# First norm of a streaming encoder step: sums of squares on another engine, smaller token tiles, loads in another order, sums in other PSUM banks

## The chip, the cores and the metric

One Trainium2 chip, one core. The metric is the device time of one execution, in microseconds (us); the program is one launch. The engines are TensorE (PE; its weight loads are PEld), VectorE (DVE), ScalarE (ACT), GpSimd (POOL) and SyncE (SP), which here only issues transfers (DMAs). Each engine works through its own queue in order.

## The reference

One layer of a streaming encoder, for 2048 prompt tokens and 32 sample tokens of width 1024:

```python
shift_m, scale_m, gate_m, shift_f, scale_f, gate_f = adaln_modulation(c, w_ada, b_ada)   # silu(c) @ w_ada + b_ada
h = rmsnorm(x, g_pre_mix) * (1.0 + scale_m) + shift_m                                     # the first norm
z = h @ w_in                        # one projection for both mixers and their gates
...                                 # chunk-band attention, gated linear attention, merge, w_out
x = x + gate_m * rmsnorm(merged @ w_out, g_post_mix)
...                                 # second norm, MLP with a causal convolution
```

All is float32. Only the first norm and the modulation that it needs (`shift_m`, `scale_m`) are touched here; the rest of the layer follows it and is about 95% of the time.

## The kernel before, in words

Everything is held transposed: 1024 channels are 8 chunks (`k`, `KD = 8`) of 128 partitions, tokens lie along the free dimension. The 2080 tokens are 5 blocks of 416 (`NB`), each of two halves of 208 (`NH`), so there are ten halves, `hb` 0 to 9. A product in float32 is made of three matmuls (`mm3`, lines 78 to 80): each operand is split into a high part (ACT) and a low part (DVE).

The first stage does these things at once:

- `ada_load(j, v)` and `ada(j, v)`: the modulation. Four pairs of loads of `w_ada` (1 MB each, tile `wa`, six buffers) give scale (`v = 1`) and shift (`v = 0`) for chunks `2j` and `2j + 1`. TensorE multiplies (L315), DVE copies the result to `mr` (L318), TensorE sums it (L322), DVE adds bias and gain (`mod_finish`, L134 and L138).
- `prep_load(hb)`: loads a half's 8 chunks as two tiles `xk` of 4 chunks (L262), six buffers.
- `prep_stats(hb, add)`: ACT squares two chunks at a time into `sq` or `sq2` (L271, L274; one buffer of `sq2`), and the engine `add` sums them (L275, L276): VectorE for halves 0 and 1, GpSimd for 2 to 9. Then `rstd_bcast` splits the sum (`sh` on ACT, `sl` on DVE, L69 and L72); its second part, `finish`, sums over partitions with two matmuls by ones (L148, L149) into a PSUM tile `pst`, and makes `rstd` (ACT L154, L155; DVE L156 to L158).
- `prep_apply(hb, r, ks)`: for each chunk, multiplies by scale and `rstd` (DVE, L294), adds the shift and rounds to the high part `hi` (ACT, L295), and makes the low part `lo` (DVE, L296), into `hA` or, past column 1664, `hB`. In half 2 the odd chunks go another way: GpSimd multiplies by the scale (`prep_scale`, L283) and by `rstd` (L292).
- `w_pieces`: two weight matrices of 256 columns, each in four pieces of two chunks (tile `wr`, two buffers, L185); ACT makes `wh` (L186), DVE `wl` (L187).
- `wave(b, ks, ps)`: the projection of block `b` by these weights, 4 outputs, chunk by chunk: 12 matmuls a chunk into four PSUM tiles `px`. `wave_evac` copies them out (`tx`, L225 on ACT, L228 on DVE) and stores them.

PSUM has two pools: `psm` with two banks, used by the stages after this one, and `psx` with six, whose tag `px` is shared here by the waves, `ada` and `pst`.

Only TensorE is in the order in which the code is written (`manual_schedule`). For the other engines and the DMA queues the framework's planner chooses the order at compile time, by readiness with its own costs, among what the buffers allow. TensorE's order for block 0 is: sums of halves 0 and 1 and the first four `ada`, then wave steps 0 to 7 with an `ada` before each of steps 1 to 4, the sum of half 2 ahead of step 4 and that of half 3 ahead of step 7. For the blocks after it there is a loop over `s_` from 2 to 9: four wave steps each, and after the first of them the sum of half `s_ + 2`, whose `prep_apply` follows; `prep_load(s_ + 4)` and `prep_stats(s_ + 3)` stand at the head.

After it, `n_tile` (L517) makes projections with tokens as rows; in its loop a side stream makes bias tables and the other modulation values.

Of the kernel before, what the change touches and what calls it, by code (L numbers as in the profile page):

```python
# [10 lines left out]
F32 = mybir.dt.float32  # L11
# [3 lines left out]
OP = mybir.AluOpType  # L15
# [5 lines left out]
KD = 8  # L21
TP, TS = 2048, 32
T = TP + TS
# [16 lines left out]
def dap(ap, offset, dims):  # L40
    return bass.AP(tensor=ap.tensor, offset=ap.offset + offset, ap=dims)


def f32(ap):
    return ap.bitcast(F32)


def parts(c0, n):

    out = []  # L50
    if c0 < TP:
        out.append((0, min(n, TP - c0), 0))
    if c0 + n > TP:
        out.append((max(0, TP - c0), n, 1))
    return out
# [3 lines left out]
def encoder_step(ctx: ExitStack, tc: tile.TileContext, I, O):  # L59
    nc = tc.nc  # L60

    def pool(st, name, bufs=1, **kw):
        return st.enter_context(tc.tile_pool(name=name, bufs=bufs, reuse_waits="tile", **kw))
# [3 lines left out]
    def split(hi, lo, src, keep=False):  # L67

        i = nc.scalar.activation(hi, src, AF.Copy)  # L69
        if keep and not in_order[0]:  # L70
            tc.keep_in_program_order(i)
        nc.vector.tensor_sub(lo, src, f32(hi))  # L72
# [22 lines left out]
    mod = consts.tile([128, 6, KD, 2], F32, name="mod")  # L95
# [44 lines left out]
    def rstd_bcast(pl, pps, tag, s, n, w, bufs=1):  # L140

        sh = pl.tile([128, w], F32R, name="sh", tag="sh")
        sl = pl.tile([128, w], F32R, name="sl", tag="sl")
        split(sh[:, :n], sl[:, :n], s)

        def finish():
            p = pps.tile([128, 512], F32, name="pst", tag=tag)
            nc.tensor.matmul(p[:, :n], ones, sh[:, :n], start=True, stop=False)  # L148
            nc.tensor.matmul(p[:, :n], ones, sl[:, :n], start=False, stop=True)  # L149

            r0 = pl.tile([128, w], F32, name="rst0", tag="sh")
            t = pl.tile([128, w], F32, name="rstt", tag="sl")
            r = pl.tile([128, w], F32, name="rstd", tag="rstd", bufs=bufs)
            nc.scalar.activation(r0[:, :n], p[:, :n], AF.Ln, bias=eps, scale=1.0 / D)  # L154
            nc.scalar.activation(r0[:, :n], r0[:, :n], AF.Exp, scale=-0.5)  # L155
            nc.vector.scalar_tensor_tensor(t[:, :n], p[:, :n], D * EPS, r0[:, :n], op0=OP.add, op1=OP.mult)  # L156
            nc.vector.scalar_tensor_tensor(t[:, :n], t[:, :n], -0.5 / D, r0[:, :n], op0=OP.mult, op1=OP.mult)
            nc.vector.scalar_tensor_tensor(r[:, :n], t[:, :n], 1.5, r0[:, :n], op0=OP.add, op1=OP.mult)  # L158
            return r[:, :n]

        return finish
# [9 lines left out]
    def h_at(x, k, c0, n):  # L171
        return hA[x][:, k, c0:c0 + n] if c0 < TA else hB[x][:, k, c0 - TA:c0 - TA + n]
# [3 lines left out]
    psm = pool(mix, "psm", bufs=2, space=PSUM)  # L176
# [14 lines left out]
    def load_w(wp, c0, n, w, kp, wr=2):  # L191
        hl_, steps = w_pieces(wp, c0, n, w, kp, wr)
        for f in steps:
            f()
        return hl_
# [40 lines left out]
    NH = 208  # L236
    late_w = {}
    with ExitStack() as st:
        stg = pool(st, "stgA", bufs=2, side="right")
        wp = pool(st, "wN", bufs=2, side="right")  # L240
        psx = pool(st, "psx", bufs=6, space=PSUM)
        prep = st.enter_context(ExitStack())
        pp = pool(prep, "prep", side="right")
# [9 lines left out]
            nc.vector.tensor_add(sel, sel, ident[:, 32 * j:32 * j + 2])  # L253

        XK = {}
        POOL = {2: (1, 3, 5, 7)}

        def prep_load(hb, q_=nc.sync):
            XK[hb] = []
            for k in range(0, KD, 4):  # L260
                x = pp.tile([128, 4, NH], F32, name="xk", tag="xk", bufs=6)
                q_.dma_start(x, dap(I["xT"], k * 128 * T + NH * hb, [[T, 128], [128 * T, 4], [1, NH]]))  # L262
                XK[hb].append(x)

        def prep_stats(hb, add):

            sq = pp.tile([128, 2, NH], F32, name="sq", tag="sq", bufs=2)
            for k in range(0, KD, 2):
                x = XK[hb][k // 4][:, k % 4:k % 4 + 2]
                if k == 0:  # L270
                    nc.scalar.activation(sq, x, AF.Square)  # L271
                    continue
                s2 = pp.tile([128, 2, NH], F32, name="sq2", tag="sq2")
                nc.scalar.activation(s2, x, AF.Square)  # L274
                add.tensor_add(sq, sq, s2)  # L275
            add.tensor_add(sq[:, 0], sq[:, 0], sq[:, 1])  # L276
            return lambda: rstd_bcast(pp, psx, "px", sq[:, 0], NH, NH, 2)

        def prep_scale(hb):
            for k in POOL.get(hb, ()):  # L280
                for a, e, s in parts(NH * hb, NH):
                    xs = XK[hb][k // 4][:, k % 4, a:e]
                    nc.gpsimd.tensor_scalar(xs, xs, mod[:, 1, k, s:s + 1], 1.0, op0=OP.mult, op1=OP.mult)  # L283

        def prep_apply(hb, r, ks_=range(KD)):
            for k in ks_:
                for a, e, s in parts(NH * hb, NH):
                    hi, lo = [h_at(x, k, NH * hb + a, e - a) for x in range(2)]
                    xs = XK[hb][k // 4][:, k % 4, a:e]
                    s1, s2 = mod[:, 1, k, s:s + 1], mod[:, 0, k, s:s + 1]  # L290
                    if k in POOL.get(hb, ()):
                        nc.gpsimd.tensor_mul(xs, xs, r[:, a:e])  # L292
                    else:
                        nc.vector.scalar_tensor_tensor(xs, xs, s1, r[:, a:e], op0=OP.mult, op1=OP.mult)  # L294
                    nc.scalar.activation(hi, xs, AF.Identity, bias=s2)  # L295
                    nc.vector.scalar_tensor_tensor(lo, xs, s2, f32(hi), op0=OP.add, op1=OP.subtract)  # L296

# [2 lines left out]
        def ada_load(j, v):  # L300

            PIECE[j, v] = []
            for half in range(2):
                w = pa.tile([128, 4, 256], F32, name="wa", tag="wa", bufs=6)
                nc.sync.dma_start(w, dap(I["w_ada"], half * 512 * 6 * D + v * D + 256 * j,
                                         [[6 * D, 128], [128 * 6 * D, 4], [1, 256]]))
                PIECE[j, v].append(w)
# [28 lines left out]
        def wave(b, ks_, ps, chunks=range(4)):  # L336
            for k in ks_:
                for i in chunks:
                    mm3(ps[i][:, :NB], [t_terms(w0[i // 2], 128 * (i % 2), b, k)], first=k == 0, last=k == KD - 1)

        def wave_tiles():
            return [psx.tile([128, 512], F32, name="px", tag="px") for _ in range(4)]

        def wave_evac(b, ps):
            for i in range(4):
                t_evac(stg, first[i // 2][0], i % 2, b, ps[i][:, :NB])

        fin0 = prep_stats(0, nc.vector)()
        ada_load(1, 1)
        for s_ in steps:  # L350
            s_[0]()
        ada_load(1, 0)
        m0 = ada(0, 1)
        r0 = fin0()
        fin1 = prep_stats(1, nc.vector)()
        m1 = ada(0, 0)
        m0()
        r1 = fin1()
# [1 line left out]
        fins = {}  # L360
        for s_ in steps:
            s_[1]()
        ada_load(2, 1)
        prep_load(2)
        m0 = ada(1, 1)
        m1()
        m1 = ada(1, 0)
        m0()
        ada_load(2, 0)
        ada_load(3, 1)  # L370
        prep_load(3)
        prep_apply(0, r0, [0, 1])
        prep_apply(1, r1, [0, 1])
        for s_ in steps:
            s_[2]()
        ada_load(3, 0)
        fins[2] = prep_stats(2, nc.gpsimd)
        wave(0, (0, ), ps)
        m1()
        m0 = ada(2, 1)  # L380
# [5 lines left out]
        wave(0, (1, ), ps)  # L386
        m0()
        m1 = ada(2, 0)
        fins[3] = prep_stats(3, nc.gpsimd)
        wave(0, (2, ), ps)  # L390
        m1()
        m0 = ada(3, 1)
# [1 line left out]
        prep_apply(1, r1, [4, 5])  # L394
        wave(0, (3, ), ps)
        m0()
        prep_scale(2)
        m1 = ada(3, 0)
        r2 = fins.pop(2)()()
        wave(0, (4, ), ps)  # L400
# [8 lines left out]
        r3 = f3()  # L409
        wave(0, (7, ), ps)  # L410
        prep_apply(3, r3)
        fins[4] = prep_stats(4, nc.gpsimd)
        wave_evac(0, ps)
        ada_st.close()
        arena2 = pool(ar2, "arena2")
# [1 line left out]
        for s_ in range(2, 10):  # L417
            b = s_ // 2
            if s_ + 4 < 10:
                prep_load(s_ + 4)  # L420
            if s_ + 3 < 10:
                fins[s_ + 3] = prep_stats(s_ + 3, nc.gpsimd)
            k0 = 4 * (s_ % 2)
            if s_ + 2 < 10:
                fin = fins.pop(s_ + 2)()
            if s_ % 2 == 0:
                ps = wave_tiles()
            if b < 4:
                wave(b, range(k0, k0 + 1), ps)
                prep_apply(s_ + 2, fin())  # L430
                wave(b, range(k0 + 1, k0 + 4), ps)
            elif s_ % 2 == 0:

                wave(b, range(KD), ps, (0, 1))
                wn = load_w(wp, 2048, 256, 272, 2, 2)
            else:
                wave(b, range(KD), ps, (2, 3))
            if s_ % 2:
                wave_evac(b, ps)
# [160 lines left out]
    with ExitStack() as st:  # L600
# [20 lines left out]
        for p in range(2):  # L621
            for x, sb in (("P", SBP), ("S", SBS)):
                s_ = gp.tile([128, 2, 128], F32, name=f"SB{x}{p}")
# [209 lines left out]
    with ExitStack() as st:  # L833
# [373 lines left out]
        s1 = ctx.enter_context(ExitStack())  # L1207
# [729 lines left out]
    xs = {}  # L1937
# [284 lines left out]
    for u, (p, grp) in enumerate(UNITS):  # L2222
        for m in range(NM[u]):
# [14 lines left out]
            if u == len(UNITS) - 1 and m == 2:  # L2238

                for i in range(KD):  # L2240
                    x = h_tile()[:, :, :SEG] if i < 4 else spare.pop(0) if i < 7 \
# [4 lines left out]
            if f2 is None and not queue and ndone[0] == NBLK:  # L2246
# [5 lines left out]
                sa, sq = [f2.tile([128, 2, SEG], F32, name=x) for x in ("saF", "sqF")]  # L2252
# [78 lines left out]
```

## Time and profile before

| | us |
|---|---|
| median of 3 runs | 3178.28 |
| lowest, highest | 3174.66, 3178.77 |
| the profiled execution, its own time | 3174.99 |
| its span, first to last instruction | 3173.3 |
| TensorE busy in the span | 3056.5 (96%) |
| VectorE, ScalarE, GpSimd busy | 2243.6, 1649.5, 263.7 |
| mean granted TensorE clock | 0.992 |

Rows of a timeline give: start, length, engine, line, operation, output <- inputs, shapes, count, and in brackets how long the engine stood idle before it and what released it. SPq and ACTq are the queues from which transfers are issued. A row of a stretch gives the busy time of each engine in it, the instructions in parentheses, the granted clock as a share of full speed, the busy share of the DMA engines and what they moved.

### The profile page before, as it was taken

To read this page: it belongs to the slowest core of one execution; us is meant where nothing else is said; L and a number is where in the kernel's file an instruction comes from. 1 tells how busy PE (TensorE), PEld (TensorE's weight loads), DVE (VectorE), ACT (ScalarE), POOL (GpSimd) and SP (SyncE) were. 2 spreads that over 40 slices of the span, in tenths; PEclk is the share of its full clock that TensorE was granted. 3 is DMA by queue.
4 is the path that set the end of the run, shared out by engine and by line. 5 is a ranking of instruction groups with operands and counts; after the bars stand their busy time and mean duration, and the time that the engine had idled before them with its cause. 6 is when DMAs were issued, how large, how long until landed. Compare 5 with 4: busy or idle time off the path is not lost. (4 is left out here: it accounts for less than half of the span.)

```text
span 3173.3 us, 56451 instructions
## 1 busy us (share of the span) xinstructions
PE 3056.5 (96%) x19748; PEld 2942.5 (93%) x19748; DVE 2243.6 (71%) x4903; ACT 1649.5 (52%) x3792; POOL 263.7 (8%) x417
## 2 busy tenths in 40 slices
PE   6999999999999999999999999999999999999997
PEld 4899999998999999988999899999999999999997
DVE  6735617774555545566577799998888778897877
ACT  4412224443554545544454655567656556576755
POOL 3201201111111111111000000000000000000001
PEclk9999999999999999999999999999999999999998
DMA  7344435554433333576457686787887667888784
GB/s 226 101 141 127 143 98 143 132 134 132 119 103 110 99 105 117 164 224 194 129 176 223 211 260 208 224 258 227 248 262 218 189 189 231 263 252 280 239 266 148
DMA packets 598799, 580.13 MB, mean 183 GB/s; under 512 B 53201, under 2 KB 527010, under 8 KB 598514
## 3 DMA queue, kind: packets, MB, share of 16 engines
q1 hardware_dynamic: 553826, 528.92, 55.6%
q10 hardware_dynamic: 44432, 47.34, 4.6%
q8 instruction: 155, 2.54, 0.3%
q14 instruction: 130, 1.06, 0.1%
q0 software_dynamic: 256, 0.26, 0.0%
HBM read 388.71 MB, written 187.65 MB: 182 GB/s over the span
## 5 line engine op out<-in xcount | busy, mean ns | idle before, releaser
L1876 PE MATMUL ad<-hA,hB 128*128 128x350 f32 (+2 forms) x1734 | 300.8, 323 | 5.3 <-DVE hB L1818 2.7
L78 PE MATMUL pm<-hA,wh 128*128 128x416 f32 x768 | 290.3, 378 | 0.0
L1876 PEld LDWEIGHTS ad<-hA,hB 128*128 128x128 f32 x1734 | 281.7, 189 | 7.3 <-ACT work L2002 3.8
L79 PE MATMUL pm<-hA,wh 128*128 128x416 f32 x768 | 269.9, 351 | 0.0
L80 PE MATMUL pm<-hA,wl 128*128 128x416 f32 x768 | 269.9, 351 | 0.0
L1818 DVE TENSOR_TENSOR hA<-raws,hA 128x512 fp32r<-128x512 f32 (+1 forms) x367 | 242.0, 668 | 12.5 <-ACT hA L1813 12.2
L1813 ACT ACTIVATE hA<-raws 128x512 fp32r<-128x512 f32 (+1 forms) x367 | 222.0, 617 | 31.7 <-DMA raws<-in_w_up_dram 10.8
L1876 PE MATMUL ad<-hA,hA 128*128 128x348 f32 (+2 forms) x1308 | 226.9, 324 | 3.0 <-ACT work L2002 2.2
L1876 PE MATMUL g<-hA,hB 128*128 128x348 f32 (+2 forms) x1248 | 217.2, 323 | 6.7 <-ACT work L1998 3.9
L1876 PEld LDWEIGHTS ad<-hA,hA 128*128 128x128 f32 x1308 | 213.1, 190 | 4.3 <-ACT work L2002 2.8
L1876 PEld LDWEIGHTS g<-hA,hB 128*128 128x128 f32 x1248 | 202.4, 188 | 9.4 <-ACT work L1998 5.0
L1876 PE MATMUL ad<-hA 128*128 128x350 f32 (+2 forms) x1173 | 204.9, 324 | 4.2 <-DVE hA L1728 4.1
L1876 PEld LDWEIGHTS ad<-hA 128*128 128x128 f32 x1173 | 191.5, 190 | 5.0 <-DVE hA L1728 4.4
L1818 DVE TENSOR_TENSOR hB<-raws,hB 128x512 fp32r<-128x512 f32 (+1 forms) x289 | 191.0, 668 | 6.7 <-ACT hB L1813 6.3
L1813 ACT ACTIVATE hB<-raws 128x512 fp32r<-128x512 f32 (+1 forms) x289 | 175.9, 617 | 26.5 <-DMA raws<-in_w_up_dram 11.6
L69 ACT ACTIVATE pth<-pp 128x256 fp32r<-128x256 f32 (+1 forms) x288 | 106.0, 374 | 145.1 <-PE pp L1023 137.8
L78 PE MATMUL pn<-wh,hA 128*128 128x256 f32 (+1 forms) x624 | 177.8, 285 | 0.0
L79 PE MATMUL pn<-wl,hA 128*128 128x256 f32 (+1 forms) x624 | 177.1, 284 | 0.0
L80 PE MATMUL pn<-wh,hA 128*128 128x256 f32 (+1 forms) x624 | 177.0, 284 | 0.0
L1985 ACT COPY g<-ad 128x348 f32<-128x348 f32 (+2 forms) x102 | 44.3, 434 | 243.1 <-PE ad L1876 155.9
L72 DVE TENSOR_TENSOR ptl<-pp,pth 128x256 fp32r<-128x256 f32 (+1 forms) x288 | 117.5, 413 | 63.6 <-ACT pth L69 61.0
L1876 PE MATMUL g<-hA,hA 128*128 128x350 f32 (+2 forms) x894 | 156.1, 323 | 3.3 <-ACT g L1985 1.7
(505 smaller groups left out, 8470.0 us busy)
## 6 DMA issues: line engine op xcount, KB each, us to landing
raws<-in_w_up_dram SPq DMA_DIRECT2D x220, 256.0 KB, 4.3
raws<-sW SPq DMA_DIRECT2D x176, 256.0 KB, 3.7
sW<-raws SPq DMA_DIRECT2D x88, 256.0 KB, 3.5
raws<-in_w_down_dram SPq DMA_DIRECT2D x80, 256.0 KB, 4.8
wr<-in_w_in_dram SPq DMA_DIRECT2D x76, 256.0 KB, 3.2
sgT<-tx ACTq DMA_DIRECT2D x80, 208.0 KB, 2.7
wa<-in_w_ada_dram SPq DMA_DIRECT2D x64, 256.0 KB, 3.0
keys<-ks SPq DMA_DIRECT2D x128, 128.0 KB, 2.8
```

Of the source, the lines that this page charges most:

```text
L69: i = nc.scalar.activation(hi, src, AF.Copy)
L72: nc.vector.tensor_sub(lo, src, f32(hi))
L78: nc.tensor.matmul(out, ah, bh, start=first and i == 0, stop=False)
L79: nc.tensor.matmul(out, ah, bl, start=False, stop=False)
L80: nc.tensor.matmul(out, al, bh, start=False, stop=last and i == n - 1)
L1813: act = nc.scalar.activation(hi[:, :n], raw(i, n), AF.Copy)
L1818: nc.vector.tensor_sub(lo[:, :n], raw(i, n), f32(hi[:, :n]))
L1876: nc.tensor.matmul(out[:, :w], l_[:, k], r_[:, k, :w], start=first and k == 0 and i == 0, stop=k == n - 1 and i == 2, skip_group_check=True)
L1985: nc.scalar.copy(g[:, 0, :w], ad[:, 0, :w])
```

## The change

Four edits, all in the first stage:

1. `prep_stats` adds on VectorE for all halves; `prep_scale` and the way of half 2's odd chunks over GpSimd are gone.
2. Tokens come in tiles of two chunks instead of four, twelve buffers instead of six (the same memory).
3. `prep_load(2)` and `prep_load(3)` are written after `ada_load(3, 0)`, the last modulation weights, instead of between the earlier ones.
4. `pst` comes from `psm` (two banks) instead of sharing `px`.

```diff
-        POOL = {2: (1, 3, 5, 7)}
...
-            for k in range(0, KD, 4):
-                x = pp.tile([128, 4, NH], F32, name="xk", tag="xk", bufs=6)
-                q_.dma_start(x, dap(I["xT"], k * 128 * T + NH * hb, [[T, 128], [128 * T, 4], [1, NH]]))
+            for k in range(0, KD, 2):
+                x = pp.tile([128, 2, NH], F32, name="xk", tag="xk", bufs=12)
+                q_.dma_start(x, dap(I["xT"], k * 128 * T + NH * hb, [[T, 128], [128 * T, 2], [1, NH]]))
...
-        def prep_stats(hb, add):
+        def prep_stats(hb):
...
-                add.tensor_add(sq, sq, s2)
-            add.tensor_add(sq[:, 0], sq[:, 0], sq[:, 1])
-            return lambda: rstd_bcast(pp, psx, "px", sq[:, 0], NH, NH, 2)
-
-        def prep_scale(hb):
...
+                nc.vector.tensor_add(sq, sq, s2)
+            nc.vector.tensor_add(sq[:, 0], sq[:, 0], sq[:, 1])
+            return lambda: rstd_bcast(pp, psm, "pm", sq[:, 0], NH, NH, 2)
...
-                    if k in POOL.get(hb, ()):
-                        nc.gpsimd.tensor_mul(xs, xs, r[:, a:e])
-                    else:
-                        nc.vector.scalar_tensor_tensor(xs, xs, s1, r[:, a:e], op0=OP.mult, op1=OP.mult)
+                    nc.vector.scalar_tensor_tensor(xs, xs, s1, r[:, a:e], op0=OP.mult, op1=OP.mult)
...
         ada_load(2, 1)
-        prep_load(2)
         m0 = ada(1, 1)
...
         ada_load(3, 1)
-        prep_load(3)
...
         ada_load(3, 0)
-        fins[2] = prep_stats(2, nc.gpsimd)
+        prep_load(2)
+        prep_load(3)
+        fins[2] = prep_stats(2)
...
-        prep_scale(2)
```

More of the change, by code (lines that the diff above doesn't have):

```diff
@@ L255, in encoder_step @@
         XK = {}
-        POOL = {2: (1, 3, 5, 7)}
         def prep_load(hb, q_=nc.sync):
             XK[hb] = []
-            for k in range(0, KD, 4):
-                x = pp.tile([128, 4, NH], F32, name="xk", tag="xk", bufs=6)
-                q_.dma_start(x, dap(I["xT"], k * 128 * T + NH * hb, [[T, 128], [128 * T, 4], [1, NH]]))
+            for k in range(0, KD, 2):
+                x = pp.tile([128, 2, NH], F32, name="xk", tag="xk", bufs=12)
+                q_.dma_start(x, dap(I["xT"], k * 128 * T + NH * hb, [[T, 128], [128 * T, 2], [1, NH]]))
                 XK[hb].append(x)
-        def prep_stats(hb, add):
+        def prep_stats(hb):
             sq = pp.tile([128, 2, NH], F32, name="sq", tag="sq", bufs=2)
             for k in range(0, KD, 2):
-                x = XK[hb][k // 4][:, k % 4:k % 4 + 2]
+                x = XK[hb][k // 2]
                 if k == 0:
@@ L274, in prep_stats @@
                 nc.scalar.activation(s2, x, AF.Square)
-                add.tensor_add(sq, sq, s2)
-            add.tensor_add(sq[:, 0], sq[:, 0], sq[:, 1])
-            return lambda: rstd_bcast(pp, psx, "px", sq[:, 0], NH, NH, 2)
-        def prep_scale(hb):
[L280 to L283, printed above, removed]
+                nc.vector.tensor_add(sq, sq, s2)
+            nc.vector.tensor_add(sq[:, 0], sq[:, 0], sq[:, 1])
+            return lambda: rstd_bcast(pp, psm, "pm", sq[:, 0], NH, NH, 2)
         def prep_apply(hb, r, ks_=range(KD)):
@@ L288, in prep_apply @@
                     hi, lo = [h_at(x, k, NH * hb + a, e - a) for x in range(2)]
-                    xs = XK[hb][k // 4][:, k % 4, a:e]
+                    xs = XK[hb][k // 2][:, k % 2, a:e]
                     s1, s2 = mod[:, 1, k, s:s + 1], mod[:, 0, k, s:s + 1]
-                    if k in POOL.get(hb, ()):
-                        nc.gpsimd.tensor_mul(xs, xs, r[:, a:e])
-                    else:
-                        nc.vector.scalar_tensor_tensor(xs, xs, s1, r[:, a:e], op0=OP.mult, op1=OP.mult)
+                    nc.vector.scalar_tensor_tensor(xs, xs, s1, r[:, a:e], op0=OP.mult, op1=OP.mult)
                     nc.scalar.activation(hi, xs, AF.Identity, bias=s2)
@@ L346, in wave_evac @@
                 t_evac(stg, first[i // 2][0], i % 2, b, ps[i][:, :NB])
-        fin0 = prep_stats(0, nc.vector)()
+        fin0 = prep_stats(0)()
         ada_load(1, 1)
@@ L354, in encoder_step @@
         r0 = fin0()
-        fin1 = prep_stats(1, nc.vector)()
+        fin1 = prep_stats(1)()
         m1 = ada(0, 0)
@@ L388, in encoder_step @@
         m1 = ada(2, 0)
-        fins[3] = prep_stats(3, nc.gpsimd)
+        fins[3] = prep_stats(3)
         wave(0, (2, ), ps)
@@ L411, in encoder_step @@
         prep_apply(3, r3)
-        fins[4] = prep_stats(4, nc.gpsimd)
+        fins[4] = prep_stats(4)
         wave_evac(0, ps)
@@ L421, in encoder_step @@
             if s_ + 3 < 10:
-                fins[s_ + 3] = prep_stats(s_ + 3, nc.gpsimd)
+                fins[s_ + 3] = prep_stats(s_ + 3)
             k0 = 4 * (s_ % 2)
```

## The prediction

> **What bounds the kernel now.** I read the views from coarse to fine: the busy table by stage, TensorE's waits inside the stage that the change touches, then the timelines of the engines around the longest of those waits. Columns of the first: stretch, length, busy time (instructions) of PE, PEld, DVE, ACT, POOL, granted clock, DMA share, GB/s.
> ```profile
> span 3173.3 us, 56451 instructions
> 0.00:160.00 160.00, 124.51 (x660) 107.48 (x661) 115.90 (x285) 77.99 (x183) 41.50 (x48) 0.96 0.53 163
> 160.00:460.00 300.00, 297.25 (x2425) 290.59 (x2424) 127.17 (x228) 67.24 (x146) 33.74 (x36) 0.99 0.41 129
> 160.12 0.28 PE L78 MATMUL pn<-wh,hA 128*128 128x256 f32 x1
> ```
> All edited code runs before 160 us: at 160.12 TensorE starts the first `n_tile` matmul. From there TensorE is busy 297.25 of the next 300 us, so it is the bound, and a start that comes x earlier ends the kernel about x earlier. Before 160 us TensorE idles 35.5 us, part of it the first loads; from 20 us on it waits for this (engine, line, what released it: us in total, times, longest):
> ```profile
> PE px L79 <- DVE hA L296: 4.4, 4, 1.7
> PE pst L148 <- ACT sh L69: 4.2, 2, 2.9
> PE px L78 <- ACT hA L295: 4.0, 3, 2.0
> PE px L78 <- ACT tx L225: 3.7, 3, 1.6
> PE pm L322 <- DVE mr L318: 2.0, 1, 2.0
> PE pst L149 <- DVE sl L72: 1.9, 3, 0.9
> PE px L80 <- DVE wl L187: 1.3, 2, 0.8
> PE pm L315 <- DMA wa<-in_w_ada_dram: 0.7, 1, 0.7
> ```
> The sum is 22.2 us. The question is which of these hang on the squares that GpSimd adds, and on the token loads. ACT's own waits (same stage) say that many do:
> ```profile
> ACT sq L274 <- POOL sq L275: 11.4, 11, 1.4
> ACT sq L271 <- DMA xk<-in_xT_dram: 10.6, 5, 6.0
> ACT sq L274 <- DMA xk<-in_xT_dram: 4.6, 3, 2.8
> ```
> Queues are in order, so a square waiting for POOL to free `sq2` holds everything behind it on ACT.
>
> **The change part by part.**
>
> *1. Adds move from POOL to DVE.* Eight halves (2 to 9) have 3 adds (L275) and 1 half add (L276) each. Columns: count, then busy us and mean ns.
> ```profile
> L275 POOL TENSOR_TENSOR sq<-sq,sq 128x416 f32<-128x416 f32 x24 | 29.6, 1231 | 40.2 <-ACT sq L274 40.0
> L275 DVE TENSOR_TENSOR sq<-sq,sq 128x416 f32<-128x416 f32 x6 | 3.6, 592 | 4.2 <-ACT sq L274 4.2
> L276 DVE TENSOR_TENSOR sq<-sq 128x208 f32<-128x208 f32 x2 | 0.7, 369 | 0.0
> L294 DVE SCALAR_TENSOR_TENSOR xk<-xk,mod,rstd 128x208 f32<-128x208 f32 x68 | 36.2, 575 | 0.4
> L296 DVE SCALAR_TENSOR_TENSOR hA<-xk,mod,hA 128x208 fp32r<-128x208 f32 x64 | 27.7, 478 | 2.5 <-ACT hA L295 2.5
> L296 DVE SCALAR_TENSOR_TENSOR hB<-xk,mod,hB 128x208 fp32r<-128x208 f32 x8 | 3.0, 426 | 0.0
> 80.00:140.00 60.00, 52.85 (x266) 49.34 (x265) 47.20 (x114) 31.61 (x78) 15.94 (x17) 0.97 0.26 73
> ```
> DVE gains 24 x 0.592 + 8 x 0.369 = 17.2 us. `prep_scale` and POOL's multiply go too; the four odd chunks of half 2 become plain L294, 4 x 0.376 = 1.5 us more. So 18.7 us of new DVE work. Against it: the eight hB forms of L296 ran while POOL was idle at 3.0/8 = 0.376 us each. The 68 L294 took 36.2 against 68 x 0.376 = 25.6, and the 64 hA forms 27.7 against 24.1: 14.2 us of stretch while POOL was at work. If POOL causes it, it goes, and DVE's net is 18.7 - 14.2 = +4.5 us; if not, +18.7. I take +4.5, because the unstretched form differs from the stretched one only in its destination tile and in POOL's idleness; about half of it, 2.2 us, on TensorE's path, since between 80 and 140 us DVE is busy 47.20 of 60 us and has room.
>
> [...]
>
> *2. What the shorter chain frees.* The first knot is around half 2's sum:
> ```profile
> 41.01 0.38 ACT L69 ACTIVATE sh<-sq 128x208 fp32r<-128x208 f32 x1 [1.90 <-POOL sq L276]
> 41.42 0.37 DVE L72 TENSOR_TENSOR sl<-sq,sh 128x208 fp32r<-128x208 f32 x1 [2.13 <-ACT sh L69]
> 41.71 0.41 DVE L318 COPY mr<-pm 128x256 f32<-128x256 f32 x1
> ```
> DVE waits 2.13 us on `sl`, ACT on POOL, and the copy `mr` that TensorE needs (its 2.0 us) stands behind. The two `wl` waits (1.3) have the same origin: the square waits held the `wh` copies on ACT. With the 0.7 of `wa` (part 3) that is 4.0 us.
>
> The second knot is the last weight piece and the last modulation value:
> ```profile
> 33.41 2.31 SPq L262 DMA_DIRECT2D xk<-in_xT_dram x2
> 35.77 2.16 SPq L185 DMA_DIRECT2D wr<-in_w_in_dram x2
> 49.26 6.38 SPq L185 DMA_DIRECT2D wr<-in_w_in_dram x4
> 53.04 0.63 ACT L186 ACTIVATE wh<-wr 128x512 fp32r<-128x512 f32 x1 [3.55 <-DMA wr<-in_w_in_dram]
> 59.48 0.71 PE L79 MATMUL px<-hA,wh 128*128 128x416 f32 x1 [1.75 <-DVE hA L296]
> 60.00:64.00 4.00, 4.00 (x14) 3.73 (x13) 4.00 (x12) 2.51 (x6) 0.84 (x1) 0.50 0.79 228
> 64.00:68.00 4.00, 3.06 (x13) 2.65 (x12) 2.78 (x5) 2.61 (x6) 2.60 (x4) 0.81 0.64 192
> ```
> `wr` has two buffers. Its third pair (35.77) stood behind half 3's tokens, which waited on SP for a free `xk`; its fourth pair (49.26) waited for the late `wl`; ACT waited 3.55 us for it, DVE's `wl` and behind it `mod` waited for ACT, and TensorE lost 2.0 + 1.75 us on `hA`, after which its clock was granted at 0.50 and 0.81: (0.50 + 0.19) x 4 = 2.8 us more. With token loads behind the weights and no POOL wait this has slack: 6.5 us.
>
> The third is half 4's norm:
> ```profile
> 71.03 3.24 POOL L275 TENSOR_TENSOR sq<-sq,sq 128x416 f32<-128x416 f32 x1 [2.41 <-ACT sq L274]
> 74.30 0.55 ACT L274 ACTIVATE sq<-xk 128x416 f32<-128x416 f32 x1 [1.45 <-POOL sq L275]
> 76.00:80.00 4.00, 3.73 (x13) 3.60 (x14) 2.10 (x4) 2.35 (x6) 2.95 (x3) 0.61 0.47 155
> ```
> One POOL add, of half 5, took 3.24 us; ACT's next square waited for it, and behind that square stood half 4's `sh`, whose sum was done. TensorE lost 2.9 (L148) + 0.7 (L149) and 0.39 x 4 = 1.6 of clock: 5.2 us. A DVE add has no such length in the trace.
>
> [...]
>
> *3. Loads of halves 2 and 3 behind `ada_load(3, 0)`.* Both are 416 KB x 2. The queue is full until about 44 us:
> ```profile
> 40.00:44.00 4.00, 2.01 (x23) 1.22 (x22) 1.34 (x5) 1.35 (x4) 0.90 (x2) 1.00 1.10 344
> 44.00:48.00 4.00, 4.00 (x35) 3.15 (x35) 2.63 (x8) 2.52 (x6) 1.81 (x2) 1.00 0.41 133
> 10.04 0.55 ACT L271 ACTIVATE sq<-xk 128x416 f32<-128x416 f32 x1 [6.00 <-DMA xk<-in_xT_dram]
> 14.68 0.36 ACT L69 ACTIVATE sh<-sq 128x208 fp32r<-128x208 f32 x1
> L262 SPq DMA_DIRECT2D xk<-in_xT_dram x20: 367/368/1036, 3.2 to 113.1; - x20
> ```
> At 344 GB/s 852 KB take 2.5 us: the weights gain 2.5 to 5 us, and half 2's tokens, until now issued ahead of half 3's (33.41), land near 42. Squares to `sh` on DVE took 10.04 to 15.04, 5.0 us, so half 2's norm can reach TensorE between 44 (squares keep up with the quarters) and 47 us. TensorE would want it at 47.66 (its time now, wave step 4) minus 4.0 = 43.7. New wait: 0.3 to 3.3; I take 2.0, nearer the middle, as a quarter (213 KB at 344 GB/s) lands every 0.6 us while an add step takes 1.2. This is what is late next. Behind that wait stand wave steps 4 to 7 on TensorE; on ACT and DVE the blocked squares and adds hold `hi`, `lo` and `mod`.
>
> *4. Tiles of two chunks.* 20 more issues x 0.368 = 7.4 us of SP, which is idle there; nothing on the path. Bytes and row lengths are the same. Each tile is freed after two chunks, so later loads start earlier; squares wait 9.2 us for loads behind the first 6.0 (10.6 + 4.6 - 6.0). Bounds 0 to 9.2 gained, on ACT; I take 0 for TensorE, because in steady state the waits named `tx` and most of `hA` come from ACT's order, which I can't foresee. The first half's squares may start up to 1 us earlier; taken as 0, as the second half's `sh` waits there for the first half's `rstd`.
>
> *5. Norm sums in `psm`.* Wave tiles keep 6 banks with 4 live; the `tx` waits (3.7) come from two banks being short, before and after. 0.
>
> Sum: 4.0 + 6.5 + 5.2 - 2.0 - 2.2 = 11.5 us less. The profiled execution took 3174.99 us (3173.3 span), 3.3 below the median of 3178.28: 3163.5 in its terms, **3167** in the median's.
>
> **The rivals.** All are told against 0.2% (6.4 us), about what this kernel's runs can tell from no change.
>
> *A: the gain is eaten by the late tokens.* DVE, which never waited for POOL except through ACT, now queues behind adds whose squares wait for loads. If the 9.2 us of load waits reach TensorE through DVE, the sum is 11.5 - 9.2 = 2.3: 3176. For it: half 2's loads are displaced to the end of a full queue. Against: half the memory comes free sooner.
>
> *B (slower): DVE becomes the bound.* If the stretch isn't POOL's, nothing of 18.7 us is given back. From 80 to 140 us run about 4.5 halves, 4.5 x 2.15 = 9.7 us more on 47.20: 95% of 60 us, the point from which DVE decides. Then 18.7 us and the 9.2 of load waits stand against parts 2's 15.7: 12 us slower, 3190. Against: the hB rows.
>
> *C: everything fits.* If ACT's order also lets the 3.7 of `tx`, the 4.6 of `hA` outside the second knot and 1.2 of `sl` go, another 9.5 us go: 21 us, 3157. For it: every `xk` comes free earlier; against: nothing in the change touches the `tx` copies.
>
> *D: half-size transfers lose bandwidth.* The nearest row is that of 40 to 44 us, where pieces of 256 KB (`wr`), 416 KB (`xk`) and 512 KB (`wa`) run mixed at 344 GB/s; if each of the 8 extra transfers of halves 0 to 3 idled the full queue for one issue, 0.37 us, that is 3 us: 3170. Against: the 256 KB pieces show no dip. [...]
>
> **How the numbers follow.** Forecast (5 to 18 us gained) 0.54; A 0.23; B 0.13; C 0.07; D 0.03. Faster by over 0.2%: nine tenths of the forecast, C and half of D, 0.57. Within 0.2%: A and the forecast's rest, 0.28. Slower: B and the rest of D, 0.15. Predicted 3167, its own range 3160 to 3173; the 8-in-10 range runs from C's 3156 into A and the near end of B, 3181.
>
> **What would show it.** Right: no POOL work before the `flip` memset; the 208-wide L294 near 0.38 us; the `mr`, `wl` and `hA` waits of 40 to 60 us gone; first `n_tile` matmul near 149 instead of 160.12. A longer wait at L148 for half 2 than 3.3 us means part 3 was mis-sized. Wrong: L294 as long as before (B); DVE waiting for ACT's squares while TensorE waits for `mr` or `mod` (A); or the 11 us visible at 160 and gone at the end, if DMA-paced side work of the next stage takes them back.

## The result, and the profile after

| | before | after |
|---|---|---|
| median of 6 runs, us | 3178.12 | 3168.35 |
| lowest, highest | 3174.66, 3178.77 | 3163.32, 3174.02 |
| ratio, 95% interval | | 0.997, 0.9959 to 0.998 |
| the profiled execution (span) | 3174.99 (3173.3) | 3167.68 (3166.0) |

The change made the kernel 9.8 us faster, 0.3%. The forecast was 3167, 11 us less, with a range of 3156 to 3181. The total came out as told, in part by luck: several terms of its sum did not, as the experiments show.

The profile after: first the span, the stretches (columns as before) and the start of the first `n_tile` matmul, which I call the landmark below.

```profile
span 3166.0 us, 56490 instructions
0.00:160.00 160.00, 132.79 (x741) 118.79 (x742) 123.03 (x335) 81.89 (x190) 1.21 (x8) 0.95 0.58 179
80.00:140.00 60.00, 57.22 (x307) 56.37 (x306) 53.29 (x160) 34.71 (x88) 0.00 (x0) 1.00 0.33 98
160.00:460.00 300.00, 296.17 (x2395) 289.38 (x2394) 121.52 (x220) 66.16 (x145) 34.83 (x39) 0.99 0.40 122
149.88 0.28 PE L78 MATMUL pn<-wh,hA 128*128 128x256 f32 x1
```

GpSimd does 1.21 us in 160, against 41.50. The landmark comes at 149.88 instead of 160.12: 10.24 us earlier. The busy times up to 160 us count 10 us of the next stage in the changed kernel; up to its own landmark VectorE is busy 114.85 us (116.02 before) and TensorE 122.67 (124.63). TensorE's waits between 20 and 160 us, 22.2 us before, are now 15.0, and they are others:

```profile
PE pst L149 <- DVE sl L72: 8.3, 4, 2.8
PE pst L148 <- ACT sh L69: 5.1, 1, 5.1
PE pm L305 <- DMA wa<-in_w_ada_dram: 1.6, 3, 0.8
```

All waits for `hA`, `tx`, `mr` and `wl` (15.4 us together) are gone. The wait for `sl`, the low part of a half's sum of squares, has grown from 1.9 to 8.3 us. VectorE's groups (count, busy us, mean ns, idle time before them) say what its work costs now:

```profile
L284 DVE SCALAR_TENSOR_TENSOR xk<-xk,mod,rstd 128x208 f32<-128x208 f32 x72 | 27.5, 429 | 0.3
L286 DVE SCALAR_TENSOR_TENSOR hA<-xk,mod,hA 128x208 fp32r<-128x208 f32 x64 | 24.3, 429 | 1.1 <-ACT hA L285 1.1
L274 DVE TENSOR_TENSOR sq<-sq,sq 128x416 f32<-128x416 f32 x30 | 17.7, 590 | 8.5 <-ACT sq L273 7.0 <-ACT sq L270 1.4
L275 DVE TENSOR_TENSOR sq<-sq 128x208 f32<-128x208 f32 x10 | 3.7, 369 | 0.1
```

The multiply of the apply (L294 before) went from 575 to 429 ns in the mean, its low part from 478 to 429. The prediction's "near 0.38 us" is busy time by count: 27.5/72 = 0.382.

The one long wait left is the norm of half 2. Its timeline, of SP's queue, ACT, VectorE and TensorE:

```profile
35.18 9.95 SPq L261 DMA_DIRECT2D xk<-in_xT_dram  x10
45.18 0.97 SPq L185 DMA_DIRECT2D wr<-in_w_in_dram  x2
43.72 0.54 ACT L270 ACTIVATE sq<-xk 128x416 f32<-128x416 f32 x1
44.30 0.55 ACT L273 ACTIVATE sq<-xk 128x416 f32<-128x416 f32 x1
45.23 1.47 DVE L284 SCALAR_TENSOR_TENSOR xk<-xk,mod,rstd 128x208 f32<-128x208 f32 x4
46.62 0.42 DVE L308 COPY mr<-pm 128x256 f32<-128x256 f32 x1
46.95 0.58 DVE L274 TENSOR_TENSOR sq<-sq,sq 128x416 f32<-128x416 f32 x1
47.56 0.55 ACT L273 ACTIVATE sq<-xk 128x416 f32<-128x416 f32 x1 [2.72 <-DVE sq L274]
50.43 0.36 ACT L69 ACTIVATE sh<-sq 128x208 fp32r<-128x208 f32 x1
50.84 0.54 PE L148 MATMUL pst<-sh,ones 128*128 128x208 f32 x1 [5.05 <-ACT sh L69]
```

ACT has squared the first two pairs of chunks by 44.85, so these tokens had landed by 43.7 and 44.3. But VectorE first does four multiplies for the block in work and the copy `mr`, and adds only at 46.95. As `sq2` has one buffer, the third square waits for that add, and the norm ends at 50.84.

### The profile page after: what moved, and what is told of

Read it like the earlier page. It is cut to its first block, busy times and chain, and to the rows that moved or that the text cites. A ratio compares the mean times of both kernels' runs of the same rounds, so it can differ in the third digit from the quotient of the medians.

```text
span 3166.0 us, 56490 instructions
## 1 busy us (share of the span) xinstructions
PE 3058.6 (97%) x19748; PEld 2947.6 (93%) x19748; DVE 2242.3 (71%) x4939; ACT 1649.1 (52%) x3792; POOL 224.2 (7%) x377
## 5 line engine op out<-in xcount | busy, mean ns | idle before, releaser
L78 PE MATMUL pm<-hA,wh 128*128 128x416 f32 x768 | 290.3, 378 | 0.0
L1802 ACT ACTIVATE hA<-raws 128x512 fp32r<-128x512 f32 (+1 forms) x367 | 222.0, 617 | 29.5 <-DMA raws<-in_w_up_dram 10.2
L78 PE MATMUL pn<-wh,hA 128*128 128x256 f32 (+1 forms) x624 | 178.1, 285 | 0.0
L1974 ACT COPY g<-ad 128x348 f32<-128x348 f32 (+2 forms) x102 | 44.3, 434 | 245.7 <-PE ad L1865 157.8
```

What stands on the lines that cost most here:

```text
L78: nc.tensor.matmul(out, ah, bh, start=first and i == 0, stop=False)
L1802: act = nc.scalar.activation(hi[:, :n], raw(i, n), AF.Copy)
L1974: nc.scalar.copy(g[:, 0, :w], ad[:, 0, :w])
```

## Experiments

All times are told against a median of the kernel before from runs on the same chip: 3179.05 for the four kernels with one edit undone; 3180.83 for edit 1 alone, the useless adds beside the real ones, half 2 early and the early split; 3179.47 for the two kernels without adds and the last two. Beside each stands the landmark of its profiled execution.

A landmark comes from one execution, and the arrival of the first tokens alone moves it. In the eleven kernels with tiles of two, all that TensorE, ScalarE and SP do up to the first square is the same and in the same order, and yet that square starts at 8.10 to 8.91 us in eight of them and at 9.73 to 9.94 in three (edit 1 undone, edit 3 undone, the early split). These are the changed kernel and the one with edit 3 undone:

```profile
8.62 0.55 ACT L270 ACTIVATE sq<-xk 128x416 f32<-128x416 f32 x1 [4.67 <-DMA xk<-in_xT_dram]
9.94 0.55 ACT L270 ACTIVATE sq<-xk 128x416 f32<-128x416 f32 x1 [5.95 <-DMA xk<-in_xT_dram]
```

The shift lasts: the first matmul on `hA` starts at 24.98 to 25.69 us in the eight and at 26.52 to 26.68 in the three. So a difference of less than about 2 us between two landmarks can't be put down to an edit.

### Which of the four edits carries the gain

Each of the first four is the changed kernel with one edit undone.

**Edit 1 undone.**

```diff
+            add = nc.vector if hb < 2 else nc.gpsimd
-                nc.vector.tensor_add(sq, sq, s2)
+                add.tensor_add(sq, sq, s2)
...
+        prep_scale(2)
```

> The kernel after, with edit 1 alone undone: squares of halves 2 to 9 are added on GpSimd again and half 2's odd chunks go over GpSimd. Landmark: the first n_tile matmul, at 160.1 us before and 149.9 us after. Theory 'chain' (the gain is GpSimd leaving the chain of squares, by its waits on ACT and by the stretch of VectorE's two-input operations): the landmark goes back to 157 or later, the 208-wide L294-type operations are about 530 us-per-thousand again (mean 550 to 590 ns against 429), total 3174 to 3179. Rival 'loads' (the gain is the order and size of the loads): landmark 150 to 153, total 3167 to 3171.

Measured: 3176.5, ratio 0.9992 (0.9983 to 1.0001), landmark 159.5. This is the kernel before again, though tiles, loads and banks are the new ones. VectorE's two groups and TensorE's waits in this kernel:

```profile
L296 DVE SCALAR_TENSOR_TENSOR xk<-xk,mod,rstd 128x208 f32<-128x208 f32 x68 | 32.5, 524 | 0.3
L298 DVE SCALAR_TENSOR_TENSOR hA<-xk,mod,hA 128x208 fp32r<-128x208 f32 x64 | 27.3, 475 | 1.6 <-ACT hA L297 1.6
```

```profile
PE pst L148 <- ACT sh L69: 7.1, 1, 7.1
PE pst L149 <- DVE sl L72: 6.2, 5, 2.4
PE px L78 <- ACT hA L297: 3.4, 1, 3.4
```

The multiplies are long again (524 ns, shorter than the 550 to 590 expected), half 2's norm is 7.1 us late, and waits for `hA` are back. Without edit 1 the other three bring 0.6 us at the landmark.

**Edit 2 undone**, tiles of four chunks.

```diff
-            for k in range(0, KD, 2):
-                x = pp.tile([128, 2, NH], F32, name="xk", tag="xk", bufs=12)
+            for k in range(0, KD, 4):
+                x = pp.tile([128, 4, NH], F32, name="xk", tag="xk", bufs=6)
```

> The kernel after, with edit 2 alone undone: token tiles of four chunks, six buffers. Theory 'chain': landmark 150 to 152 (a square waits for a load now and then, up to 9 us on ACT, mostly covered), total within 3 us of after. Rival 'loads': landmark 155 or later, because loads start only when four chunks are applied and squares on ACT and adds on VectorE wait for them.

Measured: 3166.81, ratio 0.9961 (0.9947 to 0.9975), landmark 151.2, 1.3 later than in the changed kernel; in the total no loss. ACT's first square starts at 10.08 us here, against 8.62. Three kernels with tiles of two start nearly as late, so the 1.3 is not shown to be the tiles' doing.

**Edit 3 undone**, halves 2 and 3 loaded where they were.

```diff
         ada_load(2, 1)
+        prep_load(2)
...
         ada_load(3, 1)
+        prep_load(3)
...
         ada_load(3, 0)
-        prep_load(2)
-        prep_load(3)
```

> The kernel after, with edit 3 alone undone: the loads of halves 2 and 3 stand ahead of the last modulation weights again. Theory 'chain': half 2's norm no longer keeps TensorE waiting 5.1 us (under 2 us), instead up to 3 us of waits for weights or modulation come back; landmark 147 to 152. Rival 'loads': the weights come 2.5 to 5 us later, landmark 154 or later.

Measured: 3164.36, ratio 0.9957 (0.9942 to 0.9971), landmark 151.6, 1.7 later; in the total no loss either. Of the 1.7, 1.3 is there at the first square (9.94 against 8.62), before any load that this edit moves. Half 2's wait of 5.1 falls to 0.2, and others take its place:

```profile
PE pst L149 <- DVE sl L72: 8.1, 5, 2.8
PE pm L305 <- DMA wa<-in_w_ada_dram: 3.5, 6, 0.8
PE px L78 <- ACT hA L285: 2.8, 1, 2.8
PE pst L148 <- ACT sh L69: 0.2, 1, 0.2
```

**Edit 4 undone**, the sums share `px` with the waves.

```diff
-            return lambda: rstd_bcast(pp, psm, "pm", sq[:, 0], NH, NH, 2)
+            return lambda: rstd_bcast(pp, psx, "px", sq[:, 0], NH, NH, 2)
```

> The kernel after, with edit 4 alone undone: the norm sums share the six banks of the waves again. Theory 'chain' (banks cost nothing): no wait of TensorE for tx copies, landmark 149.5 to 151. Rival 'banks': the tx waits of before (3.7 us) come back, landmark 152.5 to 155.

Measured: 3168.98, ratio 0.9977 (0.9965 to 0.9989), landmark 153.6, 3.7 later. A new wait appears in TensorE's list, three times:

```profile
PE pst L148 <- DVE tx L228: 4.1, 3, 1.7
```

A half's sum now waits until VectorE has copied out a wave's product (`tx`), since that frees the bank which `pst` gets. I had priced the banks at 0.

**Edit 1 alone**, on the kernel before.

```diff
-                add.tensor_add(sq, sq, s2)
+                nc.vector.tensor_add(sq, sq, s2)
...
-        prep_scale(2)
```

> The kernel before with edit 1 alone: all adds on VectorE, half 2's odd chunks too; loads, tiles and banks as before. If edit 1 alone carries the gain: landmark 150 to 152, total 3166 to 3170. If it needs the banks as well (undoing edit 4 in after cost 3.7 us, by the norm's tile waiting for a wave's copies): landmark 153 to 156, total 3170 to 3174, with waits of L148 for tx. If it needs the loads behind the weights: landmark past 156.

Measured: 3170.19, ratio 0.997 (0.9961 to 0.998), landmark 153.6. In the total this is the whole gain of the change; at the landmark it is 6.5 of 10.2 us, and the wait for the bank is here too:

```profile
PE px L78 <- ACT hA L285: 4.4, 2, 2.8
PE pst L148 <- DVE tx L228: 3.8, 3, 2.2
PE pst L149 <- DVE sl L72: 3.6, 3, 2.0
```

So edit 1 is what makes the kernel faster. Of edits 2 to 4 (1.3, 1.7 and 3.7 us at the landmark, each with the others in place) only the 3.7 of edit 4 is clear of the scatter, and none shows in a total beyond its interval. The four do not add: 9.6 + 1.3 + 1.7 + 3.7 = 16.3 against 10.2 us. Edits 2 to 4 together bring 0.6 without edit 1 and 3.7 with it (153.6 to 149.9).

### Why edit 1 gains: the stretch, or the waiting

Two theories: GpSimd's work lengthens VectorE's instructions (the stretch), or squares and sums wait in GpSimd's chain. The next kernels part them. The added GpSimd work reads `rstd` so that it starts when a half is ready, but nothing waits for its result.

**Adds on VectorE, and useless adds on GpSimd.**

```diff
+            if hb > 1:
+                nc.gpsimd.tensor_add(dz[:, :NH], dz[:, :NH], r)
+                for _ in range(4):
+                    nc.gpsimd.tensor_add(dz, dz, dz)
```

> The kernel after, with adds on GpSimd that nothing uses: in each prep_apply of halves 2 to 9 one of 208 and four of 288 columns, 93% of the columns that GpSimd added before, started by that half's rstd. [...] Theory 'stretch' (the two-input operations of VectorE are held while GpSimd works): the 208-wide L284-type operations go from a mean of 429 to 540-600 ns, VectorE is busy 8 to 14 us longer before 160 us, the landmark (first n_tile matmul, 149.9 in after) comes at 153 to 160. Rival 'queue' (what hurt was ACT and VectorE waiting in order for a slow chain): no stretch to speak of or one that is hidden, landmark 149.5 to 151.5.

Measured: 3183.32, ratio 1.0006 (0.9996 to 1.0017), landmark 166.2. That is 16.3 us later than in the changed kernel, and later than I expected. Up to 170 us no other engine waits for GpSimd, here or in the next kernel of this kind. VectorE's two groups, GpSimd's group, and TensorE's longest wait:

```profile
L290 DVE SCALAR_TENSOR_TENSOR xk<-xk,mod,rstd 128x208 f32<-128x208 f32 x72 | 33.0, 504 | 0.3
L292 DVE SCALAR_TENSOR_TENSOR hA<-xk,mod,hA 128x208 fp32r<-128x208 f32 x64 | 31.6, 541 | 1.4 <-ACT hA L291 1.4
L284 POOL TENSOR_TENSOR dz<-dz 128x288 f32<-128x288 f32 x32 | 22.1, 690 | 2.5
```

```profile
PE pst L149 <- DVE sl L72: 13.6, 5, 3.9
```

About 29 us of GpSimd work (22.1 + 6.6) that nobody waits for undo the whole gain: the total is that of the kernel before, within the interval. The multiplies go from 429 to 504 ns, the low parts from 429 to 541.

**No adds at all** (the sums of halves 2 to 9 are left out), **and the same with the useless GpSimd adds.**

```diff
-                nc.vector.tensor_add(sq, sq, s2)
-            nc.vector.tensor_add(sq[:, 0], sq[:, 0], sq[:, 1])
+                if hb < 2:
+                    nc.vector.tensor_add(sq, sq, s2)
+            if hb < 2:
+                nc.vector.tensor_add(sq[:, 0], sq[:, 0], sq[:, 1])
```

> The kernel after without the adds of squares of halves 2 to 9 on any engine (left out: the norms of these halves take the first two chunks' squares alone; squares, split, sums and applies all run). VectorE has 17.2 us less work and GpSimd none. If the adds cost on TensorE's path what the prediction took (about half of 4.5 us net of stretch, that is up to 9 of 17.2 without the stretch): landmark 141 to 148. If VectorE's room covers them: 148 to 150.

> The kernel after without those adds (left out as in the run without adds), with the same useless adds on GpSimd as before (93% of the columns, nothing waits for them). Against the run without adds this is the stretch alone; against the run with the adds back on GpSimd (landmark 159.5) it lacks the waiting for the chain of squares. If stretch is nearly all: landmark 154 to 160, within 3 us of 159.5. If the waiting behind the chain is the larger part: 146 to 152.

Measured: without adds 3157.77, ratio 0.9933 (0.9913 to 0.9953), landmark 142.0; with the useless GpSimd work 3175.7, ratio 0.9987 (0.9976 to 0.9997), landmark 155.4 (4.1 from 159.5, where I expected at most 3). In the first the multiplies take 430 ns, in the second:

```profile
L292 DVE SCALAR_TENSOR_TENSOR xk<-xk,mod,rstd 128x208 f32<-128x208 f32 x72 | 33.9, 517 | 0.3
L294 DVE SCALAR_TENSOR_TENSOR hA<-xk,mod,hA 128x208 fp32r<-128x208 f32 x64 | 30.4, 522 | 1.4 <-ACT hA L293 1.3
```

Four landmarks now make a sum:

| kernel | landmark | step |
|---|---|---|
| no adds | 142.0 | |
| adds on VectorE (the changed kernel) | 149.9 | the adds on VectorE: 7.9 |
| no adds, GpSimd busy for nothing | 155.4 | the stretch alone: 155.4 - 142.0 = 13.4 |
| adds on GpSimd (edit 1 undone) | 159.5 | waiting in GpSimd's chain: 159.5 - 155.4 = 4.1 |

13.4 + 4.1 - 7.9 = 9.6 us, the difference between edit 1 undone and the changed kernel (159.5 - 149.9). The split between stretch and waiting is rough. The useless adds start with the apply and lengthen its two groups by 72 x (517 - 430) + 64 x (522 - 430) ns = 12.2 us; with edit 1 undone the real ones lengthen them by 68 x (524 - 430) + 64 x (475 - 430) ns = 9.3 us. If the landmark moves in proportion, the 13.4 become 10.2 and the waiting 159.5 - 142.0 - 10.2 = 7.3, an estimate. On the other side 0.8 of the 4.1 is the first square (9.73 against 8.91). So the waiting is some 3 to 7 us, and by each reading the stretch is the larger part.

What the groups lost reached TensorE about in full: 12.2 us, with the eight `hB` forms (577 against 431 ns) 13.3, against 13.4 at the landmark. Of the 17.1 us of adds on VectorE (24 x 0.590 + 8 x 0.369) less than half did.

### What is late next, taken away

**Half 2's tokens loaded early again**, half 3's left late.

```diff
         ada_load(2, 1)
+        prep_load(2)
...
         ada_load(3, 0)
-        prep_load(2)
         prep_load(3)
```

> The kernel after with half 2's tokens loaded ahead of modulation weights (2, 0), as before; half 3's stay behind. TensorE's 5.1 us wait for half 2's sum should go to under 2 us, up to 2.5 us of waits for modulation weights come back: landmark 146 to 150. If VectorE's own order holds the sum, the wait stays at 3 to 5 us and the landmark at 149 to 151.

Measured: 3161.55, ratio 0.9943 (0.9928 to 0.9958), landmark 145.9. Half 2's wait falls from 5.1 to 0.3.

**The sum of the next half split ahead of the apply.** In the changed kernel the low part `sl` stands behind a whole `prep_apply` on VectorE (here half 3's sum, VectorE and TensorE of the changed kernel):

```profile
58.92 0.36 ACT L69 ACTIVATE sh<-sq 128x208 fp32r<-128x208 f32 x1
63.63 0.43 DVE L284 SCALAR_TENSOR_TENSOR xk<-xk,mod,rstd 128x208 f32<-128x208 f32 x1
63.98 0.36 DVE L72 TENSOR_TENSOR sl<-sq,sh 128x208 fp32r<-128x208 f32 x1
64.40 0.54 PE L149 MATMUL pst<-sl,ones 128*128 128x208 f32 x1 [2.77 <-DVE sl L72]
```

ACT's part was ready at 59.3; VectorE came to its own at 63.98, and TensorE stood for 2.77 us. The edit calls the splitting part one step earlier, before the apply, with two buffers for `sh`:

```diff
-            if s_ + 2 < 10:
-                fin = fins.pop(s_ + 2)()
...
-                prep_apply(s_ + 2, fin())
+                r = fin()
+                fin = fins.pop(s_ + 3)() if s_ + 3 < 10 else None
+                prep_apply(s_ + 2, r)
```

> The kernel after with each half's sum split (sh, sl) ahead of the half before's apply in the code, sh in two buffers, the second step of rstd in place. If the 8.3 us that TensorE waits for sl come from VectorE running a whole apply first: L149 <- sl under 2 us, landmark 143 to 147, total 3160 to 3165. If VectorE is simply the bound there (busy 53.3 of 60 us from 80 to 140), the wait moves to hA: landmark 148 to 151.

Measured: 3161.52, ratio 0.9942 (0.9923 to 0.9962), landmark 144.0. The `sl` waits are gone, 5.9 us at the landmark, though this execution is one of the three with a late first square (9.83).

**Both.**

> The kernel after with half 2's tokens loaded early and each half's split ahead of the apply before it. Each alone took the landmark from 149.9 to 145.9 and 144.0. The two waits are in different places (L148 of half 2; L149 of halves 3 to 7): if they add, 140 to 142 and total 3155 to 3160; if VectorE is the bound once both are gone, 143 to 145 with waits for hA.

Measured: 3160.36 (3157.39 to 3163.52), ratio 0.9941 (0.9927 to 0.9956), landmark 139.5, 20.6 us ahead of the kernel before. Its landmark (start and end of the `n_tile` matmuls on `hA`) and its waits:

```profile
L78 PE MATMUL pn<-wh,hA x624: 276/281/681, 139.5 to 432.1; 128*128 128x256 f32 x130, 128*128 128x272 f32 x26
```

```profile
PE px L78 <- ACT hA L285: 4.3, 2, 3.6
PE pm L305 <- DMA wa<-in_w_ada_dram: 2.6, 4, 0.8
PE px L79 <- DVE hA L286: 1.5, 2, 0.8
```

This version beats both kernels, by 0.6% against the one before; the total is just above what I expected (3155 to 3160). At the landmark the two edits add up (4.0 + 5.9 = 9.9; 10.4 measured). In the total they don't: all three lie at 0.994.

**The early split, and both halves' tokens early.**

> As the run with both, but half 3's tokens early too (where before had them). If half 3's load ahead of the last weights costs what it did in after with edit 3 undone (landmark 151.6 against 145.9 with half 2 alone early, 5.7 us): 145 to 148. If the early split hides it: 140 to 143.

Measured: 3161.11, ratio 0.994 (0.9924 to 0.9957), landmark 143.3. The wait for the modulation weights `wa` is 5.8 us here (7 times), against 2.6 with half 3's tokens late. The landmark lies between the two cases expected, nearer to the one in which the early split hides the cost. So at the landmark moving half 3's load behind the weights pays (139.5 against 143.3 us), and moving half 2's does not (139.5 against 144.0).

## Why the prediction was right, and where its terms were not

**The bound and the landmark held.** It put the first `n_tile` matmul near 149; it came at 149.88. The rule that a start x earlier ends the kernel x earlier held within a few us: 10.2 at the landmark, 8.0 at the end of the `n_tile` matmuls on `hA` (451.5 and 443.5), 7.3 between the two spans, 9.8 between the medians. Over the twelve experiments the gain at the landmark and that of the median differ by up to 6.2 us (edit 3 undone: 8.5 and 14.7); 3.1 us of this can be the traced execution of before, which was that much below its median. About 2 us were given back right behind the landmark. These are the stretches from 160 to 200 us, of before and of after:

```profile
160.00:200.00 40.00, 37.25 (x284) 35.46 (x283) 22.62 (x39) 7.46 (x16) 0.00 (x0) 0.96 0.61 194
```

```profile
160.00:200.00 40.00, 36.17 (x267) 33.83 (x266) 14.25 (x25) 4.69 (x13) 0.00 (x0) 0.91 0.49 146
```

TensorE is busy 1.1 us less and at a clock of 0.91 instead of 0.96. The prediction had named DMA-paced side work as a taker. TensorE's only waits between 150 and 260 us are for such a load, the table `tr`: 3.8 us, against 2.8 before. That makes 1.0 of the 2; that the clock makes the rest is not shown. The `n_tile` matmuls on `hA` lasted 290.1 to 293.6 us in all thirteen other kernels and 291.4 in the one before, so single executions can't settle 2 us.

**Part 1, the stretch: the cause right, its share of the path wrong.** It said that GpSimd causes the 14.2 us of stretch and that this goes; the runs with useless GpSimd work show that (429 to 504 and 541 ns with the adds on VectorE; 430 to 517 and 522 without adds, 12.2 us of stretch for 28 us of GpSimd work). What in the chip lengthens them was not shown. But the prediction netted the adds against the stretch and put half of the rest, a loss of 2.2, on TensorE's path. In fact the stretch lay on it about in full (13.4 with the useless adds, an estimated 10.2 with the real ones) and the adds less than half (7.9): a gain of 2 to 5.5. The waits suggest why: the stretched instructions are the apply, for whose `hA` or next `sl` TensorE waits (16.3 us with the useless adds on top, 13.6 + 2.1 + 0.6, against 8.3 in the changed kernel), while much of the adds fits into VectorE's idle time (without adds it is busy 47.27 of the 60 us from 80 to 140). VectorE's net was mis-sized too, told 4.5 us more and measured 1.2 less up to the landmark, because groups that the prediction left out got shorter as well: `wl` from 761 to 689 ns, `sl` from 428 to 368.

**Part 2, the three knots: gone, but worth less by themselves.** The waits for `mr`, `wl` and `hA` are gone, as told. The third knot went only in part, since `sl` took the place of `sh`. Waiting in GpSimd's chain was worth some 3 to 7 us, not 15.7: much of what I booked there was the stretch seen from TensorE. Parts 1 and 2 together are 9.6 measured, against 15.7 - 2.2 = 13.5 told.

Part 2 also took 4.4 us (2.8 + 1.6) for a lowered clock that would come back with the waits. It did not: from 20 us to the landmark the mean granted clock is 0.93, against 0.95 before, because the new waits, of 5.05 us up to 50.84 and of 2.77 us up to 64.40, were followed by a low clock in their turn:

```profile
52.00:56.00 4.00, 4.00 (x13) 3.82 (x12) 3.38 (x8) 2.69 (x7) 0.00 (x0) 0.50 0.17 35
64.00:68.00 4.00, 3.60 (x11) 3.46 (x12) 3.24 (x10) 3.00 (x7) 0.00 (x0) 0.50 0.40 107
```

The second is a cleaner case than the two that the prediction went by, in which two waits stood close together (2.04 and 1.75, 2.88 and 0.74): here one gap of 2.77 us was followed by 0.50.

**Part 3, half 2's new wait: out of its bounds.** Told 2.0, between 0.3 and 3.3; measured 5.05. The tokens came about when they were put ("near 42"; squares from 43.72). The step that failed is "squares keep up with the quarters": I looked at loads and ACT, and not at VectorE's queue, where the first add stood behind four multiplies and `mr` until 46.95. The add's inputs were ready at 44.85, so at most 2.1 of the 5.05 us are due to this; the rest, 2.9 or more, is near the upper bound told. The prediction had named a longer wait here as the sign of a wrong part 3. Edit 3 has two halves that work against each other: half 3's tokens late pay (139.5 against 143.3), half 2's late cost 4.0 (149.9 against 145.9), and the edit as a whole is not clear of the scatter.

**Late next, not foreseen:** the `sl` waits (8.3). With the adds off GpSimd the sums are ready early, and VectorE's order of apply before `sl` decides (half 3's `sh` ready at 59.3, its `sl` begun at 63.98). Splitting earlier brought 5.9.

**Part 4, tiles of two: 0 told, and no more shown.** The first square starts 1.4 us earlier than before (10.04, now 8.62), beyond the "up to 1 us" that the prediction had bounded it by. All three kernels with tiles of four start at 9.64 to 10.08, eight of eleven with tiles of two at 8.10 to 8.91, but three at 9.73 to 9.94. So smaller tiles seem to help, and one execution can't say by how much.

**Part 5, the banks: 3.7, not 0.** I had read the `tx` waits of L78 as a shortage of banks that stays, and not asked who else waits for such a copy. They went instead. Once GpSimd is out of the way the sums are ready in time, and then `pst` stands in line for a bank behind a wave's copy (L148 for `tx`: 4.1 us with edit 4 undone, 3.8 with edit 1 alone, none before). With edit 1 undone the three other edits bring only 0.6 together, so edit 1 seems to uncover this gain; edit 4 was not tried alone.

**The rivals.** *A* (late tokens) did not decide, though the mechanism exists, 5.05 us of it. *B* (VectorE becomes the bound) fell with the 429 ns; had the stretch stayed with the adds on VectorE, its direction would have been right at the landmark (the run with useless GpSimd work has it 6.1 us behind the kernel before), but not its 12 us (that total is 1.0006 of before, not clear of noise). That VectorE decides from 95% on was an estimate; with the useless adds it was busy 55.72 of the 60 us from 80 to 140 (93%), TensorE 51.11, against 53.29 and 57.22 in the changed kernel. *C* was half right: the `tx` waits and all of `hA` did go, but the `sl` waits grew by 6.4 us. *D* (small transfers) fell: from 5 to 22 us, with the queue full, the loads moved 345 GB/s in the changed kernel and 343 in the one before, with tiles of four. No run shows a loss per transfer, the 3 us of 3170 or one that would make the kernel slower. The right total thus came from terms that missed both ways, which is luck: part 1 better than told by some 4 to 8, part 5 by 3.7, part 2 worse by 8 to 12, part 3's wait by 3. These do not sum exactly, as the edits overlap.

## What to carry to other kernels

Work put on an idle GpSimd wasn't free here, where VectorE is near the path: 28 to 29 us of it that nothing waits for moved the landmark by 13.4 and 16.3 us. So compare the mean of the same VectorE instruction with GpSimd idle and at work, and price the difference where TensorE waits, not as an average. When a chain is shortened, look in the queue of each engine that serves it for what now stands ahead of its next link (here `sl` behind an apply, 63.98 instead of 59.3 us, and the first add behind four multiplies, 46.95 instead of 44.85). In this kernel a small tile that shares rotating banks with long ones cost nothing visible while it came late (no wait of L148 for `tx` before), and waited as soon as it came on time (3.8 us with edit 1 alone). And before a difference of a microsecond or two between two traces is put down to an edit, look for the first instruction at which they differ: here it was the first load, ahead of everything that was edited.

## What the runs showed of the hardware that I had not expected

GpSimd adds that nothing waits for lengthened VectorE's multiplies and low parts (430 to 517 and 522 ns without adds on VectorE, 429 to 504 and 541 with them) enough to move the landmark by 13.4 us (no adds on VectorE) and 16.3 us (with them), for 28 to 29 us of GpSimd work. Smaller transfers behind one another did not slow the queue here: 345 GB/s from 5 to 22 us with tiles of 208 KB, 343 with tiles of 416 KB in the kernel before. The first token tile came at two times that differ by 0.8 to 1.8 us between executions (first square at 8.10 to 8.91 or 9.73 to 9.94 us). And a single TensorE gap of 2.77 us was followed by a granted clock of 0.50 from 64 to 68 us.
